# Elementwise Huber loss, 8192 x 8192: row pairs in two slots, three vector and two scalar passes

## The chip, the cores and the metric

The kernel runs on one core of a Trainium2 chip. The time is the device time of one execution in microseconds (us). Three executions of the kernel before took 1873.84, 1874.82 and 1876.34 us; the median is 1874.82 us.

## The reference

Two float32 matrices of 8192 x 8192 go in, one comes out, and every element is independent:

```python
diff = pred - target
abs_diff = np.abs(diff)
return np.where(abs_diff <= 1, 0.5 * diff**2, abs_diff - 0.5)
```

Each matrix is 268.4 MB, so 536.9 MB are read and 268.4 MB are written.

## The kernel before

A tile is 128 rows by all 8192 columns: one row of 32 KB per partition, 4 MB in all. There are 64 row tiles. For each, `load(i)` brings `pred` into a buffer `a` (line 41) and `target` into a buffer `b` (line 46); there are three buffers of each. The compute goes over a tile in four chunks of 2048 columns. With d the difference and c = clamp(d, -1, 1), the loss is c*c/2 + max(|d| - 1, 0), which a chunk forms in place:

- VectorE: `a = a - b` (line 68), `b = clamp(a)` (line 69);
- ScalarE: `b = Square(b * sqrt(1/2))` (line 72), `a = Abs(a)` (line 73), `a = Relu(a - 1)` (line 74);
- VectorE, two chunks later (the list `flight`): `b = b + a` (line 65).

`store(i)` writes `b` (line 55). The order is written out by hand (`manual_schedule`), so each engine executes its instructions as the program lists them. All transfers are issued by SyncE (SP) in one queue, and SP stands at a transfer until what it waits for has happened: per turn it issues the load of `a` for tile i, the load of `b` for tile i, then the store of tile i-2. The load of `b` waits until the store of the tile that had this buffer before has landed. The store waits for the last add of its tile. In the last tile, `target` and the result go in four pieces of 1 MB.

A transfer of a tile is cut over 16 DMA engines, eight partitions each; each engine works through its own share in order, and the transfer has landed when all sixteen have reported.

Of the kernel before, what the change touches and what calls it, by code (L numbers as in the profile page):

```python
# [1 line left out]

# [4 lines left out]


@with_exitstack
def kernel(  # L10
    ctx: ExitStack,
    tc: tile.TileContext,
    pred: bass.AP,
    target: bass.AP,
    out: bass.AP,
):
    nc = tc.nc
    P = 128
    fp32 = mybir.dt.float32
    Alu = mybir.AluOpType  # L20
    Act = mybir.ActivationFunctionType
    SQRT_HALF = 0.70710678118654752

    n_rows, n_cols = pred.shape
    CH = 2048
    n_ch = n_cols // CH

    pred_t = pred.rearrange("(n p) m -> n p m", p=P)
    targ_t = target.rearrange("(n p) m -> n p m", p=P)
    out_t = out.rearrange("(n p) m -> n p m", p=P)  # L30
    n_rt = pred_t.shape[0]

    neg1 = nc.alloc_sbuf_tensor("huber_neg1", [P, 1], fp32)
    nc.gpsimd.memset(neg1.ap(), -1.0)  # L34

    pool_a = ctx.enter_context(tc.tile_pool(name="sbuf_a", bufs=3))
    pool_b = ctx.enter_context(tc.tile_pool(name="sbuf_b", bufs=3))

    def load(i):
        a = pool_a.tile([P, n_cols], fp32)  # L40
        nc.sync.dma_start(out=a, in_=pred_t[i, :, :])  # L41
        b = pool_b.tile([P, n_cols], fp32)
        pieces = n_ch if i == n_rt - 1 else 1
        w = n_cols // pieces
        for k in range(pieces):
            nc.sync.dma_start(  # L46
                out=b[:, k * w : (k + 1) * w], in_=targ_t[i, :, k * w : (k + 1) * w]
            )
        return a, b

    def store(i, b):
        pieces = n_ch if i == n_rt - 1 else 1
        w = n_cols // pieces
        for k in range(pieces):
            nc.sync.dma_start(
                out=out_t[i, :, k * w : (k + 1) * w], in_=b[:, k * w : (k + 1) * w]
            )

    flight = []

    def add(a, b):
        nc.vector.tensor_tensor(out=b, in0=b, in1=a, op=Alu.add)  # L65

    def chunk(a, b):
        nc.vector.tensor_tensor(out=a, in0=a, in1=b, op=Alu.subtract)  # L68
        nc.vector.tensor_scalar(  # L69
            out=b, in0=a, scalar1=-1.0, scalar2=1.0, op0=Alu.max, op1=Alu.min  # L70
        )
        nc.scalar.activation(out=b, in_=b, func=Act.Square, scale=SQRT_HALF)  # L72
        nc.scalar.activation(out=a, in_=a, func=Act.Abs)  # L73
        nc.scalar.activation(out=a, in_=a, func=Act.Relu, bias=neg1.ap())  # L74
        flight.append((a, b))
        if len(flight) > 2:
            add(*flight.pop(0))

    ctx.enter_context(tc.manual_schedule())
    tiles = {}  # L80
    for i in range(n_rt + 2):
        if i < n_rt:
            tiles[i] = load(i)
        if i == n_rt:
            while flight:
                add(*flight.pop(0))
        if i >= 2:
            store(i - 2, tiles.pop(i - 2)[1])
        if i < n_rt:
            a, b = tiles[i]  # L90
            for k in range(n_ch):
                sl = slice(k * CH, (k + 1) * CH)
                chunk(a[:, sl], b[:, sl])


# [1 line left out]
_INS = ['pred', 'target']  # L97
_OUTS = [((8192, 8192), 'float32')]


# [23 lines left out]
```

## Time and profile before

| | |
|---|---|
| median of three executions | 1874.82 us |
| the profiled execution: its time / its span | 1876.11 us / 1874.3 us |
| VectorE (DVE) busy | 1446.6 us, 768 instructions |
| ScalarE (ACT) busy | 1447.3 us, 769 instructions |
| DMA | 805.3 MB in 198 transfers, mean 430 GB/s |

The span runs from the first to the last instruction of the profiled execution; its own time is 1.81 us longer, and it lies 1.29 us above the median. In the lists of instructions, a row gives start, duration, engine, line and operation; in the groups, the number before the bar's end is the mean in ns, and what stands behind it is idle time before the instruction and what ended it.

### The profile page before, as it was taken

How to read it: one execution, taken by the hardware profiler on the slowest of the kernel's cores; microseconds unless marked ns; L12 is line 12 of the kernel's file. 1: busy time of each engine (PE TensorE's matmuls, PEld its weight loads, DVE VectorE, ACT ScalarE, POOL GpSimd, SP SyncE). 2: the span in 40 equal slices, each digit the busy share in tenths (PEclk: the TensorE clock that was granted, in tenths of full speed). 3: DMA queues.
4: the chain of work that ended last, by engine and by line, in shares of the span. 5: the costliest groups of instructions: out<-in, count | busy, mean ns of one | idle time of the engine just before them, and what ended most of it. 6: DMA issues, size and time to landing. Idle time of an engine off the chain costs nothing.

```text
span 1874.3 us, 2040 instructions
## 1 busy us (share of the span) xinstructions
DVE 1446.6 (77%) x768; ACT 1447.3 (77%) x769; POOL 0.3 (0%) x5
## 2 busy tenths in 40 slices
DVE  4987777878778777787787877878778787787877
ACT  4987877878778787787877878778777787777877
POOL 0000000000000000000000000000000000000000
DMA  9999999999999999999999999999999999999998
GB/s 414 425 433 431 431 434 430 433 433 434 432 433 433 432 432 433 433 432 434 432 432 434 433 431 434 432 432 434 431 433 435 426 431 430 429 434 432 424 431 368
DMA packets 28529, 805.45 MB, mean 430 GB/s; under 512 B 3169, under 2 KB 3169, under 8 KB 3169
## 3 DMA queue, kind: packets, MB, share of 16 engines
q1 hardware_dynamic: 28512, 805.32, 99.9%
q14 instruction: 17, 0.13, 0.0%
HBM read 536.87 MB, written 268.44 MB: 430 GB/s over the span
## 4 chain that ended last, share of the span: by engine, by line
DMA 77%; DVE 21%; ACT 1%; issue 0%; SPq 0%; DVEq 0%
DMA out_dram<-b 44%; DMA b<-in_target_dram 33%; DVE a L68 8%; DVE b L65 8%; DVE b L69 4%; ACT a L74 0%; ACT b L72 0%; ACT a L73 0%; SPq L41 0%; DVEq L68 0%; SPq L46 0%; DVEq L69 0%
## 5 line engine op out<-in xcount | busy, mean ns | idle before, releaser
L68 DVE TENSOR_TENSOR a<-a,b 128x2048 f32<-128x2048 f32 x256 | 585.3, 2286 | 409.5 <-DMA b<-in_target_dram 409.5
L72 ACT ACTIVATE b<-b 128x2048 f32<-128x2048 f32 x256 | 488.7, 1909 | 385.5 <-DVE b L69 385.5
L65 DVE TENSOR_TENSOR b<-b,a 128x2048 f32<-128x2048 f32 x256 | 584.7, 2284 | 1.4 <-ACT a L74 1.4
L74 ACT ACTIVATE a<-a,huber_neg 128x2048 f32<-128x2048 f32 x256 | 512.6, 2002 | 8.5
L73 ACT ACTIVATE a<-a 128x2048 f32<-128x2048 f32 x256 | 484.6, 1893 | 0.0
L69 DVE TENSOR_SCALAR b<-a 128x2048 f32<-128x2048 f32 x256 | 314.0, 1227 | 8.9
L72 ACT ACT_TABLE_LOAD x1 | 1.3, 1283 | 22.9 <-DMA b<-in_target_dram 22.9
L108 POOL MEMSET const-bfloat16-1.0<- 128x1 bf16 x1 | 0.1, 101 | 0.0
L108 POOL MEMSET const-uint8-127<- 128x1 uint8 x1 | 0.1, 101 | 0.0
L34 POOL MEMSET huber_neg<- 128x1 f32 x1 | 0.1, 98 | 0.3 <-POOLq L108 0.3
L108 POOL MEMSET const-float32-0.0<- 128x1 f32 x1 | 0.1, 98 | 0.2 <-issue 0.2
L108 POOL MEMSET const-float32-1.0<- 128x1 f32 x1 | 0.1, 98 | 0.0
## 6 DMA issues: line engine op xcount, KB each, us to landing
a<-in_pred_dram SPq DMA_DIRECT2D x64, 4096.0 KB, 36.5
b<-in_target_dram SPq DMA_DIRECT2D x63, 4096.0 KB, 19.4
out_dram<-b SPq DMA_DIRECT2D x63, 4096.0 KB, 27.2
b<-in_target_dram SPq DMA_DIRECT2D x4, 1024.0 KB, 15.3
out_dram<-b SPq DMA_DIRECT2D x4, 1024.0 KB, 8.1
```

Of the source, the lines that this page charges most:

```text
L34: nc.gpsimd.memset(neg1.ap(), -1.0)
L65: nc.vector.tensor_tensor(out=b, in0=b, in1=a, op=Alu.add)
L68: nc.vector.tensor_tensor(out=a, in0=a, in1=b, op=Alu.subtract)
L69: nc.vector.tensor_scalar(out=b, in0=a, scalar1=-1.0, scalar2=1.0, op0=Alu.max, op1=Alu.min)
L72: nc.scalar.activation(out=b, in_=b, func=Act.Square, scale=SQRT_HALF)
L73: nc.scalar.activation(out=a, in_=a, func=Act.Abs)
L74: nc.scalar.activation(out=a, in_=a, func=Act.Relu, bias=neg1.ap())
L108: nc = _bacc.Bacc("TRN2", target_bir_lowering=False, num_devices=1)
```

## The change

The work is regrouped in pairs of rows. A partition now holds two adjacent rows of `pred`, 64 KB that lie together in memory, and a transfer of such a pair is 8 MB. There are two pair slots (`pairs`) and two single-row slots for `target` (`rows`), in place of three buffers `a` and three `b`; the memory used is the same, 192 KB per partition. `target` still comes in transfers of 4 MB, 32 KB per partition, now with a distance of 64 KB between one partition's run and the next in memory.

The loss is formed as max(|d| - 1/2, c*c/2), which is the same function. The Relu pass on ScalarE falls away; the last step is one VectorE instruction with two operations (`scalar_tensor_tensor`: add -1/2, then max), which writes over `a`, so the result leaves from the pair slot. It runs one chunk later instead of two, and the last one of each row is issued before the next row begins.

SP's order in a turn j of the middle is: load pair j; load `target` for its first row; store pair j-1; load `target` for its second row. The load of a pair waits for the store of pair j-2, which had its slot; the load of a `target` row waits until the compute on this slot's earlier row is done. The first pair's first row comes in four transfers of 2 MB. In the turn before the last, the second `target` load stands ahead of the store. The last pair comes as four single rows, its first row's `pred` in a row slot and `target` in the pair slot; it is stored as one row and two half rows.

```diff
-    def add(a, b):
-        nc.vector.tensor_tensor(out=b, in0=b, in1=a, op=Alu.add)
+    def finish(a, b):
+        nc.vector.scalar_tensor_tensor(
+            out=a, in0=a, scalar=-0.5, in1=b, op0=Alu.add, op1=Alu.max
+        )
...
         nc.scalar.activation(out=a, in_=a, func=Act.Abs)
-        nc.scalar.activation(out=a, in_=a, func=Act.Relu, bias=neg1.ap())
         flight.append((a, b))
-        if len(flight) > 2:
-            add(*flight.pop(0))
+        if len(flight) > 1:
+            finish(*flight.pop(0))
+
+    def compute(a, b):
+        for k in range(n_ch):
+            sl = slice(k * CH, (k + 1) * CH)
+            chunk(a[:, sl], b[:, sl])
+        finish(*flight.pop(0))
...
+    H = M // 2
+    for lo, hi in ((0, H), (H, M)):
+        load(pairs[0][:, lo:hi], pred_p, 0, lo, hi)
+        load(rows[0][:, lo:hi], targ_p, 0, lo, hi)
+    compute_row(0, 0)
+    load(pairs[0][:, M:], pred_p, 0, M, 2 * M)
+    load_b(0, 1)
+    compute_row(0, 1)
+    for j in range(1, last):
+        load_pair(j)
+        load_b(j, 0)
+        if j == last - 1:
+            load_b(j, 1)
+            store_pair(j - 1)
+        else:
+            store_pair(j - 1)
+            load_b(j, 1)
+        compute_row(j, 0)
+        compute_row(j, 1)
+    other = pairs[last % 2]
+    load(rows[0], pred_p, last, 0, M)
+    load(other[:, :M], targ_p, last, 0, M)
+    load(other[:, M:], pred_p, last, M, 2 * M)
+    load(rows[1], targ_p, last, M, 2 * M)
+    compute(rows[0], other[:, :M])
+    compute(other[:, M:], rows[1])
+    store_pair(last - 1)
+    store(last, 0, M, rows[0])
+    for lo, hi in ((0, H), (H, M)):
+        store(last, M + lo, M + hi, other[:, M + lo : M + hi])
```

More of the change, by code (lines that the diff above doesn't have):

```diff
@@ L26, with load, load_pair, load_b @@
     n_ch = n_cols // CH
[L28 to L57, printed above, removed]
+    pred_p = pred.rearrange("(n p r) m -> n p (r m)", p=P, r=2)
+    targ_p = target.rearrange("(n p r) m -> n p (r m)", p=P, r=2)
+    out_p = out.rearrange("(n p r) m -> n p (r m)", p=P, r=2)
+    n_pr = pred_p.shape[0]
+    last = n_pr - 1
+    M = n_cols
+    pool = ctx.enter_context(tc.tile_pool(name="slots", bufs=1))
+    pairs = [
+        pool.tile([P, 2 * M], fp32, name=f"pair{k}", tag=f"pair{k}") for k in range(2)
+    ]
+    rows = [pool.tile([P, M], fp32, name=f"row{k}", tag=f"row{k}") for k in range(2)]
+    def load(dst, src, j, lo, hi):
+        nc.sync.dma_start(out=dst, in_=src[j, :, lo:hi])
+    def load_pair(j):
+        load(pairs[j % 2], pred_p, j, 0, 2 * M)
+    def load_b(j, r):
+        load(rows[r], targ_p, j, r * M, (r + 1) * M)
+    def store(j, lo, hi, src):
+        nc.sync.dma_start(out=out_p[j, :, lo:hi], in_=src)
+    def store_pair(j):
+        store(j, 0, 2 * M, pairs[j % 2])
     flight = []
-    def add(a, b):
-        nc.vector.tensor_tensor(out=b, in0=b, in1=a, op=Alu.add)
+    def finish(a, b):
+        nc.vector.scalar_tensor_tensor(
+            out=a, in0=a, scalar=-0.5, in1=b, op0=Alu.add, op1=Alu.max
+        )
     def chunk(a, b):
@@ L73, in chunk, with compute_row @@
         nc.scalar.activation(out=a, in_=a, func=Act.Abs)
-        nc.scalar.activation(out=a, in_=a, func=Act.Relu, bias=neg1.ap())
         flight.append((a, b))
-        if len(flight) > 2:
-            add(*flight.pop(0))
-    ctx.enter_context(tc.manual_schedule())
[L80 to L93, printed above, removed]
+        if len(flight) > 1:
[5 more added lines that the diff above has]
+        finish(*flight.pop(0))
+    def compute_row(j, r):
+        compute(pairs[j % 2][:, r * M : (r + 1) * M], rows[r])
+    ctx.enter_context(tc.manual_schedule())
+    H = M // 2
[28 more added lines that the diff above has]
+        store(last, M + lo, M + hi, other[:, M + lo : M + hi])
 _INS = ['pred', 'target']
```

## The prediction

> **What bounds the kernel now.** I read the page's busy times and DMA rows first, then the chain, then SP's own waits, then single landings in the trace.
>
> ```profile
> span 1874.3 us, 2040 instructions
> ...
> DVE 1446.6 (77%) x768; ACT 1447.3 (77%) x769; POOL 0.3 (0%) x5
> ...
> q1 hardware_dynamic: 28512, 805.32, 99.9%
> ```
>
> The queue's packets fill 99.9% of sixteen DMA engines' span; VectorE and ScalarE are each idle for 23% of it. In a turn of the middle the chain reads:
>
> ```profile
> 600.47 27.22 DMA out_dram<-b
> 627.69 0.02 issue
> 627.70 19.37 DMA b<-in_target_dram
> 647.08 0.03 issue
> ```
>
> A `target` load takes 19.37 us because a `pred` load of 4 MB stands before it in the queue. SP's issues give the turn:
>
> ```profile
> 629.54 0.34 SPq L55 DMA_DIRECT2D out_dram<-b  x1
> ...
> 657.58 0.33 SPq L46 DMA_DIRECT2D b<-in_target_dram  x1
> ...
> 686.68 0.33 SPq L46 DMA_DIRECT2D b<-in_target_dram  x1
> ...
> 715.73 0.33 SPq L46 DMA_DIRECT2D b<-in_target_dram  x1
> ```
>
> Turns of 29.10 and 29.05 us: three transfers of 4 MB. In the trace's landing records the last report of a transfer follows that of the transfer before it by 9.69 us (median, `pred`, `target` and output alike). The records also show sixteen reports per transfer that drift apart: at 13 us the first engine reports 0.6 us before the last, at 890 us 4.7 us, at 1854 us 6.9 us. One engine is behind all others and never runs dry; it is the bound. The even share is 192 x 9.69 = 1860.5 us. Over the 187 whole-tile intervals the slowest engine loses 9.7 us on top: 0.8 us in turns such as the one that ends at 657.58 (29.88 us), in which the trace has an 8 KB instruction fetch (at 651.5; seven turns lose about that much), and the rest in short episodes of slow packets.
>
> At the end the page shows less traffic, but not on that engine:
>
> ```profile
> 1855.00:1866.00 11.00, 9.56 (x5) 9.03 (x5) 0.00 (x0) 1.00 0.97 411
> 1866.00:1874.30 8.30, 0.42 (x1) 0.00 (x0) 0.00 (x0) 1.00 0.48 201
> ```
>
> These are stretches with the DMA share and GB/s last. The reports of the last five stores follow each other by 9.62, 2.43, 2.46, 2.40 and 2.42 us: full rate for the slowest engine, while the other fifteen wait 3 us. So the tail has nothing to gain beyond about 1 us.
>
> **The change, part by part.**
>
> *Bytes and transfers.* The bytes are the same. 198 transfers become 134; each ends in a 9 ns packet per engine: 64 x 9 ns = -0.6 us. Runs of 64 KB in place of 32 KB: four 8 KB pieces took 4 x 2.43 = 9.72 us against 9.69, and three more end packets explain 0.03; the run's length costs nothing, so 0 (at the best, 61 pair transfers x 8 runs x 1 ns = -0.5 us). The 64 KB distance between `target` runs: the trace has none. The nearest rows are the last tile's `target` pieces, 8 KB out of every 32 KB, at 2.48 + 2.44 + 2.43 + 2.48 = 9.83 us, 1.4% over; for 64 loads x 9.69 us that is up to +8.8 us. The other end is 0, the store pieces' rate (2.43). I take 0, as the four vary among themselves by as much as the excess, and keep +8.8.
>
> The Trainium skill speaks against this part: "DMA: Bandwidth & Descriptors", section "Latency and other measured facts", says that large power-of-two row distances slow copies, with 207 against 214 GB/s at 512 KiB. By that the 620 us of `target` loads would grow by 3.4%, 21 us, if 64 KB behaved like 512; no run here shows it.
>
> *VectorE and ScalarE.* ScalarE loses 256 Relu passes x 2002 ns = 512.6 us, all idle-side: it was waiting for VectorE. VectorE keeps 256 subtracts and 256 clamps, and 256 adds become 256 two-operation instructions. That form is not in the trace:
>
> ```profile
> L68 DVE TENSOR_TENSOR a<-a,b 128x2048 f32<-128x2048 f32 x256 | 585.3, 2286 | 409.5 <-DMA b<-in_target_dram 409.5
> ...
> L65 DVE TENSOR_TENSOR b<-b,a 128x2048 f32<-128x2048 f32 x256 | 584.7, 2284 | 1.4 <-ACT a L74 1.4
> L74 ACT ACTIVATE a<-a,huber_neg 128x2048 f32<-128x2048 f32 x256 | 512.6, 2002 | 8.5
> ...
> L69 DVE TENSOR_SCALAR b<-a 128x2048 f32<-128x2048 f32 x256 | 314.0, 1227 | 8.9
> ```
>
> Its bounds are 1227 ns (the clamp, also two operations, one tensor) and, as two passes, 2 x 2284 = 4568 ns. I take 2284: it reads two tensors as the add does, and the clamp's second operation made it no slower than its one tensor.
>
> The Trainium skill's "Vector Engine (DVE) Microarchitecture Reference", section "Points that are easy to get wrong", says that this instruction with two SBUF sources that aren't bf16 runs at half throughput. That would be about 4.5 us a chunk, the upper end above, and the kernel would be bound by VectorE; no row of this trace holds the form.
>
> *What the new order puts on the path.* Store j-1, and the second `target` load behind it, wait at SP until row (j-1, second) is computed. Its data lands at a time L. The DMA work already issued behind it is pair j (8 MB) and the first `target` row (4 MB): 3 x 9.69 = 29.07 us, from 0.35 us before L (last packet end to last report, 1873.03 to 1873.37). So the slowest engine is fed until L + 28.7. The compute from a cold start, by the first tile's rows:
>
> ```profile
> 22.88 2.29 DVE L68 TENSOR_TENSOR a<-a,b 128x2048 f32<-128x2048 f32 x1 [22.88 <-DMA b<-in_target_dram]
> 25.21 1.23 DVE L69 TENSOR_SCALAR b<-a 128x2048 f32<-128x2048 f32 x1
> 26.35 2.28 DVE L68 TENSOR_TENSOR a<-a,b 128x2048 f32<-128x2048 f32 x1
> 26.47 1.91 ACT L72 ACTIVATE b<-b 128x2048 f32<-128x2048 f32 x1 [2.33 <-DVE b L69]
> 28.28 1.89 ACT L73 ACTIVATE a<-a 128x2048 f32<-128x2048 f32 x1
> ```
>
> From start to start: subtract 2.33, clamp 1.14, add 2.21; Square begins 1.26 after the clamp does, Abs 1.81 after that. Finish 0 begins when Abs 0 is done, 7.3; then subtract, clamp, finish 1 at 13.0, subtract at 15.2, clamp at 17.5; Square and Abs of the last chunk end at 22.5, and the last finish at 24.85. With 0.1 from landing to subtract, the store is issued at L + 24.95 and its first packet moves 1.0 us later (0.73 to 1.73 at the start), at L + 25.95. **Margin 2.8 us** per pair: covered, by pair j and its first `target` row. The other waits have more: a pair's load waits for the store before, with a `target` load of 9.7 us behind that store as cover; a first `target` row waits for compute that ended 4 us before and has 19.4 us of pair load before it. The engines that lead by more than 2.8 us will idle at the store; they are not the bound.
>
> *Ends.* The first store waits for row (0, second), which has the same 12 MB queued behind it. At the end the last half store is issued about 1 us before the queue is empty: 0, at most +1. VectorE's instruction count is the same, so I leave its fetches and their 9.7 us of losses in.
>
> Sum against the span: 1874.3 - 0.6 = 1873.7 us, as a profiled execution 1875.5; the median of the runs lies 1.3 lower: **1874 us**.
>
> **The rivals.**
>
> *Slower, by the finish instruction.* If it takes more than 2284 ns, three of its four per row lie on the store's path; the margin of 2.8 us is used up at 0.92 us more, so from 3.2 us a chunk. At 3.5 us (clamp and add one after the other, 1227 + 2284) the row is 3.6 us longer, 0.85 over the margin, x 31 = +26: 1900. At 4.57 VectorE needs 8 x (2.33 + 1.14 + 4.5) = 63.8 us a pair against 58.1 of DMA: 13 + 32 x 63.8 + 7 = 2060. For: no row has the form. Against: the clamp's two operations run without a penalty.
>
> *Slower, by the traffic.* `target` runs at twice the distance or 8 MB transfers cost up to 1.4%: 1878 to 1883. Against: all three kinds of transfer run at the same 9.69 us.
>
> *Slower, by a smaller margin.* If issue or landing takes 2.8 us longer than read here, each further us costs 31: 1880 to 1905.
>
> *Faster.* The 9.7 us that one engine loses shrink by half or more: 1864 to 1869. For: fewer ScalarE fetches, and engines that idle at the store leave memory to the slowest. Against: the losses I can name come with fetches that don't change in number if they are VectorE's.
>
> *No effect beyond the compute,* as forecast: the DMA engine's time is the same whatever the cut.
>
> **How the numbers follow.** The measurement tells 0.2%, 3.7 us, from no change (three runs lie 2.5 us apart). No effect beyond that: 0.56. Faster: 0.18. Slower: 0.26, of it 0.11 traffic, 0.07 margin, 0.08 finish. Range 1867 to 1886: it takes in the traffic case and its +8.8 and small stalls, and leaves out 2 in 10: the finish instruction, larger stalls, and the best of the faster case. The likeliest case alone: 1871 to 1877.
>
> **What would show it.** Right: finish at 2.28 us; DMA busy near 99%; VectorE idle before each row for about 4 us with a `target` load as releaser; a pair turn of 58.1 us; engines' reports within about 3 us. Wrong: finish above 3.2 us; a 4 MB share of a `target` load away from 9.69 us; SP's store issued later than 25 us after its row landed, with the DMA share falling in every turn; the slowest engine's losses far from 9.7 us.

## The result

The changed kernel takes 1881.61 us, median of seven executions (1879.11 to 1882.38), against 1875.36 us for the kernel before, median of seven. The ratio is 1.0030, 95% interval 1.0021 to 1.0040: slower by 6 us. The profiled execution took 1881.93 us, span 1880.2 us, 5.9 us over the span before.

The page of the changed kernel, in its parts busy time, DMA queue and costliest groups:

```profile
span 1880.2 us, 1655 instructions
...
DVE 1458.2 (78%) x768; ACT 943.9 (50%) x513; POOL 0.2 (0%) x4
...
q1 hardware_dynamic: 19296, 805.31, 99.8%
...
L69 DVE TENSOR_TENSOR pair<-pair,row 128x2048 f32<-128x2048 f32 x252 | 576.0, 2286 | 281.4 <-DMA row<-in_target_dram 281.4
L64 DVE SCALAR_TENSOR_TENSOR pair<-pair,row 128x2048 f32<-128x2048 f32 x252 | 576.6, 2288 | 119.1 <-ACT pair L74 119.1
```

Compute is what was foreseen: the new last step takes 2288 ns, ScalarE is down by 503 us, and VectorE waits 281.4 us in 62 waits for `target` rows, 4.5 us before each row. The DMA engines are as full as before. The time is lost inside that 99.8%.

One turn, from the list of instructions of SP and VectorE (start, duration, engine, line, operation, and in brackets idle time before it and what ended it):

```profile
852.41 0.33 SPq L44 DMA_DIRECT2D pair<-in_pred_dram  x1
...
862.11 2.29 DVE L69 TENSOR_TENSOR pair<-pair,row 128x2048 f32<-128x2048 f32 x1 [4.27 <-DMA row<-in_target_dram]
...
884.64 2.29 DVE L64 SCALAR_TENSOR_TENSOR pair<-pair,row 128x2048 f32<-128x2048 f32 x1 [1.58 <-ACT pair L74]
886.96 0.34 SPq L53 DMA_DIRECT2D out_dram<-pair  x1
887.40 0.38 SPq L44 DMA_DIRECT2D row<-in_target_dram  x1
...
910.49 0.33 SPq L44 DMA_DIRECT2D pair<-in_pred_dram  x1
```

The row landed at 862.09 (the landing record), its store was issued 24.87 us later, and this turn took 58.08 us from one pair load to the next. The next turn took 58.98. From the landing of the first pair store (91.67) to that of the last one in the loop's common order (1731.47) lie 28 turns of 58.56 us on average, where 58.14 us (six shares of 9.69) would be the even rate.

The landing records say which engine pays. For each transfer they hold sixteen reports, one per DMA engine. Below, for the changed kernel: when SP issued the transfer, when the last engine reported, the time since the last report of the transfer before, and by how much the first and the fifteenth engine were ahead of the last.

```
issue    transfer             last report  since   first  fifteenth ahead by
857.87   row <- target           891.15     9.69    3.0     2.3
886.96   out <- pair             910.47    19.33    2.4     1.6
887.40   row <- target           920.18     9.70    2.3     1.6
910.49   pair <- pred            939.51    19.34    2.2     1.6
916.08   row <- target           949.96    10.45    3.0     2.3
945.04   out <- pair             969.45    19.49    2.6     2.2
```

In the load issued at 916.08, which stands before a store, the slowest engine alone loses 0.76 us: the others' distance to it jumps from 1.6 to 2.3 and more. The trace has such a loss packet by packet in the turn at 650 us: while the other fifteen end their loads and begin the store (653.56 to 654.22), the slowest engine's last load packet but one takes 2047 ns instead of 1213.

Below, "loss" is the time by which the slowest engine falls behind the even rate, that is, by which the last report comes later than 9.69 us per 4 MB after the one before it. Summed over the whole run it is 9.5 us before and 15.7 us after. The difference, 6.2 us, covers the 5.9 us between the spans. By the step at which it falls:

| step on the queue | before: steps, loss | after: steps, loss |
|---|---|---|
| load, then a load | 68, -0.2 us | 68, -0.4 us |
| load, then a store | 62, 4.1 us (0.07 each) | 31, 11.1 us (0.36 each) |
| store, then a load | 61, 5.7 us | 30, 5.1 us |
| greatest distance first to last engine | 7.6 us | 3.4 us |

In the kernel before, 2.7 of the 4.1 us ahead of stores come in the first 330 us, while the engines are less than 3.3 us apart; later they are further apart and such losses are rare. In the changed kernel they never get further apart than 3.4 us, because the wait of the store holds the faster ones back, and the losses go on to the end.

Of the 11.1 us ahead of stores, 2.4 us lie in one step of another kind, in the turn before the last. There it is the second `target` load that waits for compute, with 2.9 us of work left ahead of it for the slowest engine, and all sixteen engines lose the time together. The other 30 steps lose 8.7 us, 0.29 each.

### The profile page after: what moved, and what is told of

Read it like the earlier page. It is cut to its first block, busy times and chain, and to the rows that moved or that the text cites. A ratio compares the mean times of both kernels' runs of the same rounds, so it can differ in the third digit from the quotient of the medians.

```text
span 1880.2 us, 1655 instructions
## 1 busy us (share of the span) xinstructions
DVE 1458.2 (78%) x768; ACT 943.9 (50%) x513; POOL 0.2 (0%) x4
## 3 DMA queue, kind: packets, MB, share of 16 engines
q1 hardware_dynamic: 19296, 805.31, 99.8%
## 4 chain that ended last, share of the span: by engine, by line
DMA 56%; DVE 29%; ACT 12%; SPq 1%; issue 1%; ACTq 0%; DVEq 0%
DMA row<-in_target_dram 53%; DVE pair L64 11%; DVE pair L69 11%; ACT row L73 6%; DVE row L70 6%; ACT pair L74 6%; DMA out_dram<-pair 2%; DMA pair<-in_target_dram 1%; SPq L53 1%; DVE row L69 0%; DVE row L64 0%; ACT row L74 0%; DVE pair L70 0%; SPq L44 0%; ACT pair L73 0%
## 5 line engine op out<-in xcount | busy, mean ns | idle before, releaser
L73 ACT ACTIVATE row<-row 128x2048 f32<-128x2048 f32 x252 | 480.2, 1906 | 900.3 <-DVE row L70 900.3
L69 DVE TENSOR_TENSOR pair<-pair,row 128x2048 f32<-128x2048 f32 x252 | 576.0, 2286 | 281.4 <-DMA row<-in_target_dram 281.4
L64 DVE SCALAR_TENSOR_TENSOR pair<-pair,row 128x2048 f32<-128x2048 f32 x252 | 576.6, 2288 | 119.1 <-ACT pair L74 119.1
L74 ACT ACTIVATE pair<-pair 128x2048 f32<-128x2048 f32 x252 | 477.1, 1893 | 0.0
L70 DVE TENSOR_SCALAR row<-pair 128x2048 f32<-128x2048 f32 x252 | 309.1, 1227 | 8.7
L73 ACT ACTIVATE pair<-pair 128x2048 f32<-128x2048 f32 x4 | 7.6, 1905 | 11.4 <-DVE pair L70 11.4
L64 DVE SCALAR_TENSOR_TENSOR row<-row,pair 128x2048 f32<-128x2048 f32 x4 | 9.2, 2288 | 1.9 <-ACT row L74 1.9
L69 DVE TENSOR_TENSOR row<-row,pair 128x2048 f32<-128x2048 f32 x4 | 9.1, 2286 | 1.4 <-DMA pair<-in_target_dram 1.4
L74 ACT ACTIVATE row<-row 128x2048 f32<-128x2048 f32 x4 | 7.6, 1893 | 0.0
L70 DVE TENSOR_SCALAR pair<-row 128x2048 f32<-128x2048 f32 x4 | 4.9, 1227 | 0.1
## 6 DMA issues: line engine op xcount, KB each, us to landing
pair<-in_target_dram SPq DMA_DIRECT2D x1, 4096.0 KB, 19.4
```

The costliest lines, as they stand in the source:

```text
L64: nc.vector.scalar_tensor_tensor(out=a, in0=a, scalar=-0.5, in1=b, op0=Alu.add, op1=Alu.max)
L70: nc.vector.tensor_scalar(out=b, in0=a, scalar1=-1.0, scalar2=1.0, op0=Alu.max, op1=Alu.min)
```

## The experiments

The margin of a store is the time from its first packet to the moment at which the slowest engine would have run out of work that is queued ahead of it; "cover" means the same for any transfer. Theory 1: the store's margin of 2.8 us holds the engines together, and at that distance the slowest one loses time at each step from a load to a store, though it never runs dry. Theory 2: the new traffic (64 KB runs, 64 KB distances, 8 MB transfers) costs by itself. Theory 3 came up after the first runs: compute's own work beside the DMA costs the time.

**Split store.**

```diff
         load_pair(j)
+        store(j - 1, 0, M, pairs[(j - 1) % 2][:, :M])
         load_b(j, 0)
-        if j == last - 1:
-            load_b(j, 1)
-            store_pair(j - 1)
-        else:
-            store_pair(j - 1)
-            load_b(j, 1)
+        store(j - 1, M, 2 * M, pairs[(j - 1) % 2][:, M:])
+        load_b(j, 1)
```

> The changed kernel, with each 8 MB store of the middle cut into its two rows; the first row's store is issued before the load of the first target row, and only the second row's store waits for the row computed last. Behind that wait now lie 8 + 4 + 4 MB instead of 8 + 4, so the margin grows from 2.8 to about 12.5 us. Theory 1, the short margin (it holds the engines together at a distance of 2.3 to 3.3 us, and at that distance the slowest engine loses some tenths of a us at each turn, where in the kernel before it drifts off to 7 us and the losses end): the distance of the engines' reports grows past 5 us, the losses of the slowest engine over the even share fall from 15.7 to about 10 us, 1875 to 1877 us. Theory 2, the traffic (64 KB runs and 64 KB distances cost by themselves): loads are the same, 1880 to 1882 us.

Measured: 1882.95 us (1.0041, 1.0029 to 1.0054). The total says theory 2, the records don't: 7.8 of the 16.7 us of loss lie in one place, the load of the last pair's first row, which stood behind a wait for compute with too little queued ahead of it. My edit had moved that place. In the rest, the distance grew to 7 us and the loss ahead of a store fell to 0.10 us a step. The margin of the second row's store is 7.1 us here and not 12.5: the two `target` rows of a pair now land 19.4 us apart instead of 29, so the second row's compute begins late.

**Late store in the kernel before.**

```diff
-        if len(flight) > 2:
+        if len(flight) > 4:
...
+        if extra:
+            nc.vector.tensor_tensor(out=b, in0=b, in1=b, op=Alu.max)
```

`extra` holds for the last chunk of each tile but the last; the added instruction leaves the values as they are.

> The kernel before, with its adds two chunks later (flight deeper by two) and one more pass of 2.2 us over the last chunk of each tile that changes no value, so that each store is issued 13.5 us later: its margin falls from 16 to 2.6 us, all transfers as before. Theory 1, the short margin: the distance of the engines' reports stays at about 3 us, losses of the slowest engine rise by 4 to 10 us, 1879 to 1885 us. Theory 2, the traffic: no change but for one more instruction fetch at most, 1874 to 1877 us, and the distance may still be held at 3.

Measured: 1919.06 us (1.0233, 1.0219 to 1.0247), far more than expected. The distance stayed at 3.5 us or less and the loss ahead of stores was 21.0 us, as theory 1 has it, but 8 us were lost in one stall while the pipeline filled and about 10 us at the end. The run was repeated without these.

**Late store, middle tiles only.** The same two edits, where `late` holds:

```diff
-        if len(flight) > 2:
+        while len(flight) > (4 if late else 2):
...
+            late = 4 <= i < n_rt - 4
             for k in range(n_ch):
                 sl = slice(k * CH, (k + 1) * CH)
-                chunk(a[:, sl], b[:, sl])
+                chunk(a[:, sl], b[:, sl], late, late and k == n_ch - 1)
```

> The kernel before with its stores 13.5 us late (margin 2.6 us), in tiles 4 to 59 alone, so that the start and the end run as in the kernel before; the first such kernel lost some 18 us in two stalls there. All transfers are those of the kernel before. Theory 1: distance of the reports held near 3 us, losses of 0.3 to 0.5 us per turn at the step from the target load to the store, 56 turns, +17 to +28 us: 1892 to 1903 us. Theory 2, the traffic (pairs, runs, distances): not present here, 1874 to 1877 us.

Measured: 1898.98 us (1.0133, 1.0118 to 1.0147). All transfers are those of the kernel before, in the same order, and no wait of the slowest engine is longer than what is queued for it. The stretches 850 to 908 and 908 to 966 us (length; busy time of VectorE, ScalarE and GpSimd; granted TensorE clock, DMA share, GB/s), of the kernel before:

```profile
850.00:908.00 58.00, 45.21 (x24) 45.20 (x24) 0.00 (x0) 1.00 1.00 433
908.00:966.00 58.00, 45.21 (x24) 45.20 (x24) 0.00 (x0) 1.00 1.00 431
```

and of this kernel:

```profile
850.00:908.00 58.00, 48.60 (x26) 44.14 (x25) 0.00 (x0) 1.00 1.00 424
908.00:966.00 58.00, 48.49 (x27) 44.09 (x24) 0.00 (x0) 1.00 0.99 416
```

The DMA engines are as busy by their share and move 2 to 3.5% less. The loss ahead of stores is 20.1 us in 62 steps, 0.32 each, of 32.1 us in all; the changed kernel has 0.36, or 0.29 without the step in its turn before the last. This comes without pairs, long runs or wide distances, so theory 2 doesn't explain it.

**Short compute in the changed kernel.**

```diff
-        nc.scalar.activation(out=b, in_=b, func=Act.Square, scale=SQRT_HALF)
-        nc.scalar.activation(out=a, in_=a, func=Act.Abs)
+        nc.scalar.activation(
+            out=b[:, :16], in_=b[:, :16], func=Act.Square, scale=SQRT_HALF
+        )
+        nc.scalar.activation(out=a[:, :16], in_=a[:, :16], func=Act.Abs)
```

and likewise for the last step.

> The changed kernel, but Square, Abs and the last step run over 16 columns of each chunk instead of 2048 (the rest of the output is the plain difference). All transfers, their order and the number of instructions are the same; a row takes about 16 us instead of 24.9, so the margin is 11 us instead of 2.8. Theory 1, the short margin: the distance of the engines' reports grows past 5 us, 1874 to 1877 us. Theory 2, the traffic: 1880 to 1882 us.

Measured: 1873.44 us (0.9989, 0.9980 to 0.9998): with the changed kernel's transfers in the changed kernel's order, 8 us less than the changed kernel and no slower than the kernel before. The distance grew to 7.5 us; the loss ahead of stores was 0.10 us a step. The margin, read from the trace, is 12.9 us. The 62 `target` loads at 64 KB distance lost 2.4 us in all. Theory 2 falls. What this run couldn't exclude is theory 3, as compute was cut with the margin.

**Margin of 4.9 us and of 0.9 us.** Two kernels with the same transfers as the changed one and small edits of compute:

```diff
+            if k == 0:
+                flight[-1] = tuple(t[:, :16] for t in flight[-1])
```

> The changed kernel, but the last step of each row's first chunk runs over 16 columns instead of 2048 (the rest of that chunk keeps |d|). All transfers and the number of instructions are the same; the row is 2.1 us shorter, margin 4.9 us instead of 2.8. Theory 1, the short margin: the distance of the reports reaches 4 to 5 us, the loss per step from a load to a store falls from 0.36 to about 0.1 us, 1873 to 1876 us. If a margin of 11 us as in the run with short compute is needed: 1878 to 1881 us. Theory 3 (compute's own traffic costs the difference): 1880 to 1882 us, as only a twelfth of VectorE's work is gone.

```diff
-            chunk(a[:, sl], b[:, sl])
+            chunk(a[:, sl], b[:, sl], k in (1, 2))
```

Where the third argument is true, the clamp runs twice.

> The changed kernel with a second clamp, which changes no value, in the second and third chunk of each row: the row is some 1.9 us longer, margin about 0.9 us instead of 2.8. All transfers the same. Theory 1: the distance of the reports is held at 1 to 2 us, the loss per step stays at 0.3 us or more, and the slowest engine itself may now run dry here and there, 1882 to 1892 us. Theory 2 (traffic): nothing until the margin is gone, 1880 to 1883 us.

Measured: 1875.26 us (1.0006, 0.9997 to 1.0014) with 4.9 us, and 1905.72 us (1.0159, 1.0145 to 1.0173) with 0.9 us, more than expected. The same stretches of 58 us, first with 0.9 us, then the changed kernel, then with 4.9 us:

```profile
850.00:908.00 58.00, 48.21 (x27) 28.57 (x16) 0.00 (x0) 1.00 0.98 417
908.00:966.00 58.00, 48.31 (x28) 27.65 (x16) 0.00 (x0) 1.00 0.98 416
```

```profile
850.00:908.00 58.00, 45.37 (x25) 29.39 (x16) 0.00 (x0) 1.00 1.00 428
908.00:966.00 58.00, 44.76 (x25) 28.64 (x17) 0.00 (x0) 1.00 1.00 430
```

```profile
850.00:908.00 58.00, 41.45 (x24) 29.40 (x17) 0.00 (x0) 1.00 1.00 434
908.00:966.00 58.00, 41.33 (x24) 29.27 (x17) 0.00 (x0) 1.00 1.00 432
```

ScalarE's work is untouched and VectorE's is less by 132 us of 1458 in the run with 4.9 us (1326.3), yet 6 of the 8 us come back: theory 3 falls. The four kernels with one and the same traffic, ordered by margin as the traces show it (0.35 us from the last packet to the last report of the load ahead, 1.0 us from the issue of the store to its first packet):

| margin of the store | time | greatest distance of the engines | loss of the slowest engine in all | of it ahead of stores | of that in the turn before the last |
|---|---|---|---|---|---|
| 0.7 us (0.9 planned) | 1905.72 us | 2.5 us | 41.3 us | 4.9 us | 3.1 us |
| 2.8 us (the change) | 1881.61 us | 3.4 us | 15.7 us | 11.1 us | 2.4 us |
| 4.9 us | 1875.26 us | 5.3 us | 8.8 us | 6.6 us | 0.5 us |
| 12.9 us (11 planned) | 1873.44 us | 7.5 us | 6.4 us | 3.0 us | 0.0 us |

The time follows the margin, and so does the step in the turn before the last, whose load has the same cover as the stores. The way from the margin to the loss that theory 1 gives is not borne out at every point. With 4.9 us the loss ahead of stores is 0.21 us a step, twice what was expected, and steps of 0.3 to 1.0 us still occur at distances of 4 to 5 us. With the least margin the engines are closest together, yet the loss ahead of stores is smaller than in the changed kernel. There the loss falls elsewhere than expected: 22.4 us in the load right behind the store, of 1.0 to 1.8 us in 13 of 29 turns, 10.0 us in the stores themselves, and 4.2 us at the end, where the last half store came too late.

**Split store, mended.** In full compute, a larger margin can be had by cutting the store. The first attempt to mend the end keeps the changed kernel's order in the last turn:

```diff
-        load_b(j, 0)
         if j == last - 1:
+            load_b(j, 0)
             load_b(j, 1)
             store_pair(j - 1)
         else:
-            store_pair(j - 1)
+            store(j - 1, 0, M, pairs[(j - 1) % 2][:, :M])
+            load_b(j, 0)
+            store(j - 1, M, 2 * M, pairs[(j - 1) % 2][:, M:])
             load_b(j, 1)
```

> The split store again, with the turn before the last in the changed kernel's order (both target rows, then the pair's store whole), because the first try ran dry for 7.8 us there: the load of the last pair's first row stood at SP behind compute with too little queued before it. Theory 1, the short margin: full compute, same loads, margin 12.5 us in 29 of 31 turns; the distance of the reports grows past 3.5 us, losses of the slowest engine 8 to 10 us as in the middle of the first try, 1874 to 1876 us. Theory 3, that the run with short compute was faster because idle engines leave SBUF to the DMA: compute is full here, so 1880 to 1882 us.

Measured: 1878.78 us (1.0022, 1.0013 to 1.0030), with 4.9 us lost in one place again (the load of the turn before the last, 14.58 us after the transfer before it instead of 9.69). The second:

```diff
-        load_b(j, 0)
         if j == last - 1:
+            load_b(j, 0)
+            store_row(j - 1, 0)
             load_b(j, 1)
-            store_pair(j - 1)
+            store_row(j - 1, 1)
         else:
-            store_pair(j - 1)
+            store_row(j - 1, 0)
+            load_b(j, 0)
+            store_row(j - 1, 1)
             load_b(j, 1)
```

`store_row(j, r)` stores row r of pair j.

> The split store with the stall of the second try mended: there the second target row of the turn before the last waited at SP for compute with 29 us queued before it where 30 were needed (rows start closer together once the store is cut), and 4.9 us were lost at one place. Now a 4 MB store stands before it, and all waits have cover. Theory 1, the short margin: no loss over 1.5 us at any one place, losses of the slowest engine 6 to 9 us in all, 1873 to 1876 us. Theory 3 (full compute beside the DMA costs the difference to the run with short compute) or 2 (traffic): 1879 to 1882 us.

Measured: 1876.15 us median of twelve (1872.73 to 1883.88), 1.0010, 1.0001 to 1.0019. It stands 1.3 us above the kernel before of its own round, where the changed kernel stood 6.3 us above, with nothing left out of the computation. Here too the second row's store has a margin of about 7.7 us, not 12.5. But the executions lie 11 us apart, two to four times as far as those of the kernels with whole stores. The profiled one was the slowest of them: the loss ahead of stores was 0.23 us a step, at distances of 4 to 7 us too, where theory 1 has no losses. Cutting the store doubles the number of such steps (61 against 31). So a larger margin lowers the time, but a wide distance of the engines is no guard against the losses; what decides when a step loses time stays open.

**Wide chunks.** A second cause was named in the prediction: turns of the kernel before in which an instruction fetch costs the slowest engine 0.8 us.

```diff
-            for k in range(n_ch):
-                sl = slice(k * CH, (k + 1) * CH)
+            w, depth = (CH, 2) if i == n_rt - 1 else (2 * CH, 1)
+            for k in range(n_cols // w):
+                sl = slice(k * w, (k + 1) * w)
...
-        if len(flight) > 2:
+        while len(flight) > depth:
```

> The kernel before with chunks of 4096 columns instead of 2048 in all tiles but the last (and the adds one chunk later instead of two), so that VectorE and ScalarE have about half the instructions and half the instruction fetches. If each fetch of VectorE's instructions costs the slowest engine 0.8 us, as six turns of the kernel before suggest: 2.4 to 3.2 us less, 1871 to 1873 us, with three such turns left. If the coincidence is chance: 1874 to 1876 us and six or seven such turns.

Measured: 1871.53 us median of eleven (1871.04 to 1873.39), 0.9984, 0.9975 to 0.9993: it beats both kernels. In the kernel before, six stores lose 0.80 to 0.81 us, each 6 us after a fetch (the fetch at 651.47 us, the landing at 657.56 us), and the packet right behind the fetch takes 1687 ns instead of 1213. Here such turns are all gone, not half of them, and the engines' distance stays at 3.5 to 4.1 us from 350 us on. Ten fetches are left, and no store behind them lands late by 0.8 us. That the slower turns went because none of the ten met the engine that is last is likely, but not shown.

The same in the split store, first with chunks of 4096 in all pairs but the first and the last, then in pairs 1 to 27 alone and with the mended order (the edit shown):

```diff
-        compute(pairs[j % 2][:, r * M : (r + 1) * M], rows[r])
+        w = 2 * CH if 0 < j < last - 3 else CH
+        compute(pairs[j % 2][:, r * M : (r + 1) * M], rows[r], w)
```

> The same with chunks of 4096 columns in all rows but those of the first and the last pair, so about half the instructions. Theory 1 and the fetches together: the 0.8 us turns with a fetch fall from six or seven to none or three, 1870 to 1873 us. If the wide chunks' gain in the kernel before was something that belongs to its order: 1874 to 1876 us.

> The same with chunks of 4096 columns in the rows of pairs 1 to 26. Short margin gone and half the fetches: no or three turns with 0.8 us, 1870 to 1873 us, level with the wide chunks in the kernel before. If the wide chunks' gain belongs to the order of the kernel before: 1873 to 1876 us.

Measured: 1878.91 us (1.0030, 1.0016 to 1.0044) for the first, with 6.1 us in the same stall as above, and 1877.72 us (1.0014, 1.0002 to 1.0026) for the mended one, of eleven executions between 1870.08 and 1883.18. No gain over the split store with narrow chunks: the losses ahead of stores, 12.9 us in the profiled execution, swallow it.

## Why the prediction was wrong

It said no change, 1874 us; it is 6 us slower, within the range of 1867 to 1886 us.

*What bounds the kernel* held: one DMA engine that is behind the others and never runs dry. All of the 6 us are time that this engine loses. Of the seven turns of 0.8 us that were put down to fetches, six have one; the seventh, 0.73 us at 239 us, is a load ahead of a store.

*Bytes and transfers* held. 64 KB runs cost nothing: the 30 pair loads, 8 MB each, are 0.7 us faster in all than the even rate. The 64 KB distance cost at most the 2.4 us of the short-compute run over 62 loads, 0.4%, and not the 1.4% of the upper bound. The Trainium skill's "DMA: Bandwidth & Descriptors", section "Latency and other measured facts", gives a loss at a row distance of 512 KiB (207 against 214 GB/s); at 64 KB these runs show no loss of that size.

*VectorE and ScalarE* held: 2288 ns against the 2284 taken. The half throughput that the Trainium skill's "Vector Engine (DVE) Microarchitecture Reference", section "Points that are easy to get wrong", gives for this form isn't seen here; the measurement decides.

*The new order on the path* held in its numbers for the middle: store 24.87 us after the landing (24.95 predicted), margin 2.8, engines within 3.4 us (about 3), ends at full rate (4.84 and 4.83 us for the last two half stores).

The step that failed is the conclusion drawn from them: "The engines that lead by more than 2.8 us will idle at the store; they are not the bound", and with it the sum's "I leave its fetches and their 9.7 us of losses in". I took the losses of the slowest engine for a constant of the kernel. The runs show that they depend on the margin: 15.7 us at 2.8 us of margin against 9.5 us in the kernel before (9.7 in the prediction's count), and, with the changed kernel's own transfers, 8.8 us at 4.9 us and 6.4 us at 12.9 us. 2.4 of the 15.7 us fall in the turn before the last, whose second `target` load waits with the same short cover; the prediction has no term for it. That the margin acts through the distance between the engines fits the middle of the changed kernel, but isn't shown. The rival that named the margin had the right place and the wrong mechanism: it priced only a slowest engine that runs dry, 31 us per us beyond 2.8, and gave nothing for a margin that is met.

A hint was in the landing records of the kernel before. Up to 385 us, while the engines were close, the loss ahead of stores was 2.7 us in 12 steps, 0.23 each; after that it was 1.3 us in 50. At 0.23 us the 31 steps of the changed kernel would come to 7 us instead of 4.1, an estimate that has nearly half of the 7 us that were added there; the 0.36 us itself only the changed kernel shows.

## What to carry to other kernels

In a kernel bound by DMA, a wait that is covered by 2.8 us isn't free: sixteen engines share a transfer and drift apart, and here it took 4.9 us of cover to come back within 1 us of the kernel before. So ask of each store or load that waits for compute how much is queued ahead of it, and not only whether the slowest engine is still fed. Fewer and larger transfers bought nothing here; fewer, wider instructions did buy 3.5 us.

## What the runs showed of the hardware

- Runs of 8, 16, 32 and 64 KB per partition move at nearly one rate: packets of 309, 611, 1213 and 2418 ns.
- A load followed by a load cost the slowest engine nothing in the kernel before and in the changed one (68 steps each, together -0.6 us). A load followed by a store did, in the middle by up to 0.9 us, on one engine, while the others had begun to store. Whether the others' writes slow its reads, or the step itself, no run here separates.
- In the changed kernel's turn before the last, where two `target` loads follow each other and a store comes next, all sixteen engines together lost 2.4 us (packets of up to 2484 instead of 1213 ns). The same step lost 3.1 us with 0.7 us of cover, 0.5 us with 4.9 us and nothing with 12.9 us; why all engines slow down is open.
- An 8 KB instruction fetch can cost a DMA engine 0.8 us, though its own packet takes 0.31: in the six turns of the kernel before the packet behind it takes 0.42 to 0.48 us more. In the kernel before, a fetch at 545.51 us is followed by such a packet (1635 ns), but the last report of that turn came on time; it shows in the time, as far as these records go, only if it is the engine that is last.
